# A hard-max attention kernel: load times, step spacing and gather allowance

## The chip, the cores and the metric

The kernel runs on one core of one Trainium2 chip. The metric is the device time of one execution in microseconds (us). A profiled execution comes with a trace; its span, from the first to the last instruction, is a little shorter than the time of the execution.

## The reference

```python
def reference(q, k, v):          # q, k, v: (4, 4096, 128) float32
    logits = np.matmul(q, k.transpose(0, 2, 1))
    best = np.argmax(logits, axis=-1)
    b_idx = np.arange(q.shape[0])[:, None]
    return v[b_idx, best, :].astype(np.float32)
```

For each of 4 × 4096 queries the kernel finds the key with the largest dot product and returns that key's row of v. There is no softmax: the result is a gather.

## The kernel before, in words

The keys of a batch are taken in groups of four rows. From each group the kernel builds sums and differences on TensorE (`trn_half` for the first batch, `unit_k` for the others, L195), so that the largest dot product of a group of four comes out of absolute values and maxima. The queries are cut into 128 tiles of 128 rows (T = 128), 32 to a batch. The work on one tile goes through these stages, spread over several turns of the loop `for it in range(T)` (L792):

- **Screen** (`screen`, `dpart`, `spart`, L228 to L256). TensorE forms 128 × 1024 scores of differences (pd), ScalarE (ACT) takes their absolute value (A, L234, two a tile), TensorE adds A to the scores of sums (psn), ACT writes one half out as 16-bit integers (E, L247). The PSUM pool has four buffers.
- **Fold and top** (`fold` L258, `top` L263). VectorE (DVE) takes the maximum of psn and E into W, whose other half-words hold group numbers, and then the eight largest of 1024 (TOP). Fold of tile it−1 and top of tile it−2 are in turn it.
- **Gather** (`gather`, L271). For four tiles together (two from tile 108 on), DVE computes the indices of the best groups (cand); for each tile one indirect DMA issued by GpSimd (POOL) fetches the three key differences of the best group (kg, L282) from a DRAM copy k16.
- **Dots** (`dots`, L290). DVE multiplies kg by the query (prod, in pieces of two tiles), folds the products twice (p1, p2) and reduces them to D. After each instruction the generator yields. `("dve",)` lets it go on at the next call of `step`; `("wait", 1)` only in the next turn of the loop. `step(it)` (L712) is called twice a turn, once before and once after `top`, and advances one dots generator (two if two are ready) and each pick by an instruction; from TAIL (turn 74) on, picks by two.
- **Pick** (`pick`, L313). For a chunk of eight tiles (four from tile 96 on) five small DVE instructions (mx, near, sel, CNT, win) choose the row within the group; `put_values` then queues one indirect DMA a tile, the value gather (vr, L342), in `late_q`, and a store of the rows by the SP queue.
- **Flags.** Queries whose leading candidates are too close are listed and computed again exactly: `flag_segment` for the first 64 tiles, in the loop from turn 75 on; `flags_last` (L466) for the last 64, after the loop. The latter ends with gathers FK, FQ, FV and a scatter into the output (L541). `late(LATE)` issues that many queued value gathers before FK, `late(1 << 20)` the rest after it.

The order of instructions on every engine is the order of this Python code; nothing reorders it later. POOL issues all gathers and the loads of keys and queries one after the other. How many value gathers go into a turn is decided by `issue(it)` (L743): kg gathers first, one a turn (two when many are queued); then `room` grows by `rate` less `busy` and shrinks by what was issued, capped at 3, and up to two value gathers go out while it is at least 1.

The keys and queries in natural order lie in natk and natq (two buffers each, b % 2). Batch 1's keys are loaded in turns 0 to 7; after that batch b+1's queries are loaded in turns 10 to 16 of a batch, batch b+2's keys in turns 18 to 24. `put_first` (DVE makes kd, SP stores it three times) and `add_rest` (POOL, an accumulating DMA) make k16 for the next batch, in turns 9, 13 and 13, 17 of a batch. `turn_q` transposes queries by SP; `unit_k` runs in the first part of the batch before.

Of the kernel before, what the change touches and what calls it, by code (L numbers as in the profile page):

```python
# [8 lines left out]
FP16 = mybir.dt.float16  # L9
# [12 lines left out]
TAU = 8.0  # L22
NEAR = 0.5
SLOTS = 6
LATE = 4
NKG = 6


# [1 line left out]
def kernel(ctx, tc, q, k, v, out):  # L30
    nc = tc.nc
    B, Sq, D = q.shape
    Sk = k.shape[1]
    P = 128
    NQT = Sq // P
    T = B * NQT
# [9 lines left out]
    bp = ctx.enter_context(tc.tile_pool(name="kq", bufs=1))  # L46
# [10 lines left out]
    k16 = [dr.tile([Sk, 96], FP16, name=f"k16_{b}") for b in range(B)]  # L57
    kT = [bp.tile([P, Sk], FP16, name=f"kT{i}", tag=f"kT{i}") for i in range(2)]
    qT = [bp.tile([P, Sq], FP16, name=f"qT{i}", tag=f"qT{i}") for i in range(2)]
    natk = [bp.tile([P, 2, 16, P], FP16, name=f"natk{i}", tag=f"natk{i}") for i in range(2)]  # L60
    kd = bp.tile([P, 2, 4, 3, P], FP16, name="kd", tag="kd")
    natq = [bp.tile([P, NQT, P], FP16, name=f"natq{i}", tag=f"natq{i}") for i in range(2)]

    def load_k(b, h, x, y):
        kb = k[b].rearrange("(h p n) d -> p h n d", p=P, n=16)
        nc.gpsimd.dma_start(out=natk[b % 2][:, h, x:y], in_=kb[:, h, x:y])  # L66

    def load_q(b, x, y):
        nc.gpsimd.dma_start(out=natq[b % 2][:, x:y], in_=q[b].rearrange("(p t) d -> p t d", p=P)[:, x:y])  # L69

    def put_k(b, h):
        if b >= B:
            return
        src = natk[b % 2][:, h].rearrange("p (g f) d -> p g f d", f=4)
        nc.vector.tensor_tensor(out=kd[:, h], in0=src[:, :, 1:4, :], in1=src[:, :, 0:1, :].to_broadcast([P, 4, 3, P]),
                                op=OP.subtract)
        kb16 = k16[b].rearrange("(h p n) d -> p h (n d)", p=P, n=16)
        nc.sync.dma_start(out=kb16[:, h], in_=kd[:, h].rearrange("p g f d -> p (g f d)"))

    def put_first(b, h):  # L80
        if b >= B:
            return
        src = natk[b % 2][:, h].rearrange("p (g f) d -> p g f d", f=4)
        nc.vector.tensor_scalar(out=kd[:, h, :, 0, :], in0=src[:, :, 0, :], scalar1=-1.0, scalar2=None, op0=OP.mult)
        kb16 = k16[b].rearrange("(r x) d -> r (x d)", x=4).rearrange("(h p g) (f d) -> p h g f d", h=2, p=P, f=3)
        for f in range(3):
            nc.sync.dma_start(out=kb16[:, h, :, f, :], in_=kd[:, h, :, 0, :])

    def add_rest(b, h):
        if b >= B:  # L90
            return
        src = natk[b % 2][:, h].rearrange("p (g f) d -> p g f d", f=4)
        kb16 = k16[b].rearrange("(r x) d -> r (x d)", x=4).rearrange("(h p g) (f d) -> p h g f d", h=2, p=P, f=3)
        nc.gpsimd.dma_start(out=kb16[:, h].rearrange("p g f d -> p g (f d)"), in_=src[:, :, 1:4, :].rearrange("p g f d -> p g (f d)"),
                            accum_op=OP.add)

    def load_part(b, i, n=8):
        if b >= B:
            return
        if i < 8:  # L100
            load_k(b, i // 4, i % 4 * 4, i % 4 * 4 + n)
        else:
            load_q(b, (i - 8) * NQT // 8, (i - 8 + n // 4) * NQT // 8)

    load_k(0, 0, 0, 16)
    load_q(0, 0, 4)
# [14 lines left out]
    identh = cp.tile([P, P], FP16, tag="identh")  # L121
# [73 lines left out]
    def unit_k(b, i):  # L195
        h, u, y = i // 8, i // 2 % 4, i % 2
        x = 2 * (u // 2)
        ps = pp.tile([P, 256], FP32, tag="u", name=f"uk_{b}_{i}")
        for m in (2 * y, 2 * y + 1):
            o = ps[:, (m - 2 * y) * P:(m - 2 * y + 1) * P]  # L200
            nc.tensor.matmul(out=o, lhsT=natk[b % 2][:, h, 4 * m + x, :], rhs=identh, start=True, stop=False)  # L201
            nc.tensor.matmul(out=o, lhsT=natk[b % 2][:, h, 4 * m + x + 1, :],  # L202
                             rhs=identn if u % 2 else identh, start=False, stop=True)
        c = u * 1024 + h * 512 + y * 256
        nc.scalar.activation(out=kT[b % 2][:, c:c + 256], in_=ps, func=AF.Copy)  # L205

    def turn_q(b, x, y):
        nc.sync.dma_start_transpose(out=qT[b % 2][:, x * P:y * P].rearrange("p (t r) -> p t r", r=P),
                                    in_=natq[b % 2][:, x:y, :].rearrange("p t d -> p (t d)"))

    def trn_q(x, y, put):
        ps = pp.tile([P, 512], FP32, tag="u", name=f"tq_{x}")
# [77 lines left out]
    def dots(c, x, m):  # L290
        c0 = chunks[c][0]
        d = D_t[c % 4]
        b = x // NQT
        gap = ("wait", 1) if m == 4 and x < 200 else ("dve",)
        yield "until", lambda: ("kg", x) in done, 2 if m < 4 and x < TAIL else 1
        kg = kg_t.pop(x)
        prod = rp.tile([P, 4, 3, P], FP16, tag="prod", name=f"prod_{x}")[:, 0:m]
        h = min(m, 2)
        for i in range(0, m, h):
            nc.vector.tensor_tensor(out=prod[:, i:i + h], in0=kg[:, i:i + h],  # L300
                                    in1=natq[b % 2][:, x + i - b * NQT:x + i + h - b * NQT, :].unsqueeze(2).to_broadcast([P, h, 3, P]),
                                    op=OP.mult)
            yield gap
        p1 = rp.tile([P, 4, 3, 64], FP16, tag="p1", name=f"p1_{x}")[:, 0:m]
        nc.vector.tensor_tensor(out=p1, in0=prod[:, :, :, 0:64], in1=prod[:, :, :, 64:128], op=OP.add)  # L305
        yield gap
        p2 = rp.tile([P, 4, 3, 32], FP16, tag="p2", name=f"p2_{x}")[:, 0:m]
        nc.vector.tensor_tensor(out=p2, in0=p1[:, :, :, 0:32], in1=p1[:, :, :, 32:64], op=OP.add)  # L308
        yield "dve",
        nc.vector.tensor_reduce(out=d[:, x - c0:x - c0 + m, 1:4], in_=p2, axis=AX_X, op=OP.add)  # L310
        done.update(("dot", i) for i in range(x, x + m))
# [154 lines left out]
    def flags_last(t0, t1, ready, fill, late):  # L466
# [47 lines left out]

        late(LATE)
        get(FK[:, 0, :], k_flat, gb[:, 0:1], B * Sk)
# [226 lines left out]
    def issue(it):  # L743
        n = 0
        clock[0] = it
        put_out(it)
        behind = len([g for g in near_q if g not in marks]) > (2 if it >= TAIL else 4)
        while near_q and (n < 1 + behind or near_q[0] in marks or it >= T - 1):
            g = near_q.pop(0)
            n += g not in marks  # L750
            g()
        if fast and it >= rest[0]:
            fast.pop(0)()
            rest[0] = it + 2
            n += 1
        if it < 16:
            take_late(2 if n == 0 and len(late_q) > 4 else 1)
            return
        b, qt = it // NQT, it % NQT
        busy = 0.7 if qt % 2 == 0 and (10 <= qt < 18 and b + 1 < B or 18 <= qt < 26 and b + 2 < B) else 0.0  # L760
        if qt in (13, 17) and b + 1 < B:
            busy += 1.0
        rate = 2.42 if it < 72 else 2.5 if it < 100 else 2.42
        room[0] = min(room[0] + rate - busy, 3.0) - n
        for i in range(2):
            if room[0] >= 1 and late_q and it < T - 1:
                take_late(1)
                room[0] -= 1
# [16 lines left out]
            start(flag_segment(0, t + 1, lambda: ("cnt", last) in done, lambda: ("out", last) in done), "flags")  # L785

    TAIL = T - 54
    units = []
    for b in range(1, B):
        x = b * NQT  # L790
        units += [(x - 1, x - NQT + (6 + 3 * i // 2 if b == 1 else 1 + 2 * i), unit_k, b, i) for i in range(16)]
    for it in range(T):  # L792
        b, qt = it // NQT, it % NQT
        if it < 8:
            load_part(1, it, 4)
        elif 10 <= qt < 18 and qt % 2 == 0:
            load_part(b + 1, qt - 2)
        elif 18 <= qt < 26 and qt % 2 == 0:
            load_part(b + 2, qt - 18)
        open_units = [u for u in units if u[1] <= it]  # L800
        if open_units:
            u = min(open_units)
            units.remove(u)
            assert it <= u[0]
            u[2](*u[3:])
        if it == 1:
            turn_q(0, 4, 8)
        if it == 40:
            nc.sync.dma_start(out=q32, in_=q[B - 1].rearrange("(p t) d -> p t d", p=P)[:, NQT - 2:NQT])
        if it in (1, 2, 3):  # L810
            turn_q(0, it * 8, it * 8 + 8)
        elif qt >= 16 and qt % 2 == 0 and b + 1 < B:
            turn_q(b + 1, (qt - 16) * 2, (qt - 14) * 2)
        if it > 0:
            screen(it)
        if it >= 1:
            fold(it - 1)
        if it == 1:
            put_k(0, 1)
        if it % NQT in (9, 13):  # L820
            put_first(it // NQT + 1, it % NQT // 13)
        if it % NQT in (13, 17):
            add_rest(it // NQT + 1, it % NQT // 17)
        step(it)
        if it >= 2:
            top(it - 2)
        step(it)
        if it >= 2:
            gathers(it - 2)
        issue(it)  # L830

    def flush():
# [73 lines left out]
```

## Time and profile before

| | before |
|---|---|
| time, median of 3 executions | 443.18 us (442.71 to 443.21) |
| span of the profiled execution | 441.9 us |
| PE busy | 378.9 us |
| DVE busy | 405.9 us |
| ACT busy | 375.6 us |
| POOL busy | 306.2 us |
| kg gathers (L282) | 126, mean 1003 ns |
| value gathers (L342) | 126 and two for the last two tiles, mean 999 ns |
| fold (L260) / top (L264) on DVE | 1306 / 1227 ns mean |
| A (L234) / E (L247) on ACT | 1046 / 1036 ns mean |
| first and last fold start | 16.8 and 404.2 us |

Busy time is the sum of an engine's instructions; two neighbours on DVE or ACT can overlap by about 0.1 us, so a stage is better read from start to start. POOL's time between two gathers is not counted as busy. The page also cuts the span into 40 slices of 11 us, each digit the busy tenths of an engine.

### The profile page before, as it was taken

The page shows a single profiled execution, that of the slowest core. Times are in us where ns is not written, and L with a number is a line of the kernel's source. Part 1 is how long each engine was busy: PE and PEld are TensorE (multiplying, and loading weights), DVE is VectorE, ACT ScalarE, POOL GpSimd, SP SyncE. Part 2 cuts the span into 40 slices and gives each one's busy share as a digit, 9 for nine tenths or more (in the row PEclk, how much of TensorE's full clock was granted, in tenths as well). Part 3 has the DMA queues.
Part 4 walks back from the last instruction along what each step waited for, and adds up shares of the span by engine and source line. Part 5 has one row for each costly group of instructions (what it writes and reads, how often), then busy time and mean ns, then how long its engine had stood idle before and what let it go on. Part 6 is the DMA issues. An engine that isn't in the chain of part 4 may idle for free.

```text
span 441.9 us, 6163 instructions
## 1 busy us (share of the span) xinstructions
PE 378.9 (86%) x1830; PEld 168.0 (38%) x1830; DVE 405.9 (92%) x734; ACT 375.6 (85%) x437; POOL 306.2 (69%) x335
## 2 busy tenths in 40 slices
PE   7999999999999999999998889999889997892100
PEld 4444444444444444444443334443333333330100
DVE  2688999999999999999999999999999999999840
ACT  2899999999999999999998889999989998892000
POOL 8413456677768786777777776777777777777673
PEclk9999999999999999999999999999999999998555
DMA  7933999463326999743336993453322332323432
GB/s 123 202 101 65 157 148 139 106 130 80 108 58 134 180 163 170 147 114 91 84 94 142 173 162 100 96 132 107 85 82 84 90 89 80 88 80 102 122 113 53
DMA packets 52868, 50.54 MB, mean 114 GB/s; under 512 B 34136, under 2 KB 40890, under 8 KB 52832
## 3 DMA queue, kind: packets, MB, share of 16 engines
q0 software_dynamic: 19072, 33.87, 39.2%
q1 hardware_dynamic: 33760, 16.26, 14.5%
q8 instruction: 14, 0.23, 0.2%
q14 instruction: 22, 0.18, 0.2%
HBM read 40.05 MB, written 14.55 MB: 124 GB/s over the span
## 4 chain that ended last, share of the span: by engine, by line
ACT 37%; issue 20%; DVE 13%; PE 12%; POOL 8%; DMA 8%; POOLq 0%; ACTq 0%; DVEq 0%; SPq 0%
ACT A L234 31%; ACT E L247 6%; DVE TOP L264 4%; PE psn L225 4%; POOL vr L342 4%; PE pd L225 4%; POOL kg L282 4%; DVE W L260 4%; PE psn L244 3%; DMA vr<-in_v_dram,win 3%; DMA natk<-in_k_dram 2%; DMA out_dram<-vr 1%; DMA kg<-k,cand 1%; DVE prod L300 1%; DMA vr<-in_v_dram,win_w 1%
## 5 line engine op out<-in xcount | busy, mean ns | idle before, releaser
L234 ACT ACTIVATE A<-pd 128x1024 f16<-128x1024 f32 x256 | 260.8, 1046 | 12.5 <-PE pd L225 12.0
L282 POOL DMA_INDIRECT kg<-k,cand x126 | 126.4, 1003 | 80.0 <-DVE cand L276 48.7
L260 DVE SCALAR_TENSOR_TENSOR W<-psn,E 128x1024 int16<-128x1024 f32 x128 | 167.1, 1306 | 7.4 <-ACT E L247 5.3
L225 PE MATMUL psn<-kT,qT 128*128 128x512 f16 x512 | 151.9, 378 | 11.4 <-ACT A L234 4.0
L225 PE MATMUL pd<-kT,qT 128*128 128x512 f16 x512 | 151.9, 379 | 8.7 <-ACT A L234 8.2
L264 DVE MAX8 TOP<-W 128x8 f32<-128x1024 f32 x128 | 157.0, 1227 | 0.0
L225 PEld LDWEIGHTS <-qT 128*128 128x128 f16 x1024 | 97.9, 97 | 151.8 <-issue 62.0
L342 POOL DMA_INDIRECT vr<-in_v_dram,win x126 | 125.9, 999 | 40.0 <-issue 36.1
L244 PE MATMUL psn<-A,identh 128*128 128x512 f16 x512 | 152.1, 378 | 0.0
L247 ACT ACTIVATE E<-psn 128x1024 int16<-128x1024 f32 x128 | 132.6, 1036 | 2.3 <-PE psn L244 1.5
L244 PEld LDWEIGHTS <-identh 128*128 128x128 f16 x512 | 49.6, 97 | 60.7
L300 DVE TENSOR_TENSOR prod<-kg,natq 128x768 f16<-128x768 f16 x63 | 34.8, 554 | 0.4 <-DMA kg<-k,cand 0.4
L205 ACT ACTIVATE kT<-uk 128x256 f16<-128x256 f32 x48 | 20.6, 429 | 1.5 <-PE uk L202 1.5
L305 DVE TENSOR_TENSOR p<-prod 128x768 f16<-128x768 f16 (+1 forms) x36 | 18.1, 502 | 0.1
L310 DVE TENSOR_REDUCE D<-p 128x12 f32<-128x384 f16 (+1 forms) x36 | 17.7, 492 | 0.1
L201 PE MATMUL uk<-identh,natk 128*128 128x128 f16 x96 | 15.8, 218 | 0.0
L484 PE MATMUL fp_e<-n_e,tri 128*128 128x1 f32 x2 | 0.6, 364 | 13.5 <-DVE n_e L482 13.5
L202 PEld LDWEIGHTS <-natk 128*128 128x128 f16 x96 | 9.3, 97 | 7.2 <-issue 5.1
L308 DVE TENSOR_TENSOR p<-p 128x384 f16<-128x384 f16 (+1 forms) x36 | 11.9, 330 | 0.1
L66 POOL DMA_DIRECT2D natk<-in_k_dram x19 | 11.3, 599 | 0.8 <-POOLq L890 0.8
L201 PEld LDWEIGHTS <-natk 128*128 128x128 f16 x96 | 9.3, 98 | 5.6
L69 POOL DMA_DIRECT2D natq<-in_q_dram x15 | 9.2, 614 | 0.0
(152 smaller groups left out, 140.1 us busy)
## 6 DMA issues: line engine op xcount, KB each, us to landing
out_dram<-vr SPq DMA_DIRECT2D x31, 256.0 KB, 2.1
natq<-in_q_dram POOLq DMA_DIRECT2D x12, 256.0 KB, 5.3
natk<-in_k_dram POOLq DMA_DIRECT2D x10, 256.0 KB, 4.5
k<-kd SPq DMA_DIRECT2D x18, 128.0 KB, 3.7
k<-natk POOLq DMA_DIRECT2D x6, 384.0 KB, 6.4
kg<-k,cand POOLq DMA_INDIRECT x126, 3.0
vr<-in_v_dram,win POOLq DMA_INDIRECT x126, 2.7
natk<-in_k_dram POOLq DMA_DIRECT2D x8, 128.0 KB, 5.7
```

Of the source, the lines that this page charges most:

```text
L201: nc.tensor.matmul(out=o, lhsT=natk[b % 2][:, h, 4 * m + x, :], rhs=identh, start=True, stop=False)
L205: nc.scalar.activation(out=kT[b % 2][:, c:c + 256], in_=ps, func=AF.Copy)
L225: nc.tensor.matmul(out=ps[:, n * 512:(n + 1) * 512], lhsT=qT[b % 2][:, qt * P:(qt + 1) * P], rhs=kT[b % 2][:, u * 1024 + n * 512:u * 1024 ...
L234: nc.scalar.activation(out=A, in_=ps, func=AF.Abs)
L244: nc.tensor.matmul(out=ps[:, n * 512:(n + 1) * 512], lhsT=identh, rhs=A[:, n * 512:(n + 1) * 512], start=False, stop=True)
L247: nc.scalar.activation(out=E, in_=ps, func=AF.Relu, scale=QSCALE)
L260: nc.vector.scalar_tensor_tensor(out=W_t[t % NW].bitcast(I16)[:, 1::2], in0=ps, scalar=QSCALE, in1=E, op0=OP.mult, op1=OP.max)
L264: nc.vector.max(out=TOP[:, t, :], in_=W_t[t % NW].bitcast(FP32))
L282: near_q.append(lambda j=j: nc.gpsimd.indirect_dma_start(out=kg[:, j].rearrange("p f d -> p (f d)"), out_offset=None, in_=k16[t0 // NQT], ...
L300: nc.vector.tensor_tensor(out=prod[:, i:i + h], in0=kg[:, i:i + h], in1=natq[b % 2][:, x + i - b * NQT:x + i + h - b * NQT, :].unsqueeze(2 ...
L305: nc.vector.tensor_tensor(out=p1, in0=prod[:, :, :, 0:64], in1=prod[:, :, :, 64:128], op=OP.add)
L342: late_q.append(lambda j=j: nc.gpsimd.indirect_dma_start(out=vr[:, j, :], out_offset=None, in_=v_flat, in_offset=IOA(ap=win[:, i + j:i + j ...
```

## The change

The buffers natk and natq get a third copy (b % 3). The loads of batches 1 to 3 follow a table, `load_plan(batch, first turn, gap, pieces, what)`; `put_first` and `add_rest` get turns of their own by batch. In the old code batch 3's keys were loaded in turns 50 to 56 and its queries in 74 to 80, its `put_first` in 73 and 77, `add_rest` in 77 and 81. `dots` waits a turn between instructions only for x < 80, and in the last 20 turns `step` is called a third time. The allowance has other rates. LATE goes from 4 to 5.

```diff
-LATE = 4
+LATE = 5
...
-    natk = [... for i in range(2)]
+    natk = [... for i in range(3)]
...
-    natq = [... for i in range(2)]
+    natq = [... for i in range(3)]
...
-        gap = ("wait", 1) if m == 4 and x < 200 else ("dve",)
+        gap = ("wait", 1) if m == 4 and x < 80 else ("dve",)
...
-        busy = 0.7 if qt % 2 == 0 and (10 <= qt < 18 and b + 1 < B or 18 <= qt < 26 and b + 2 < B) else 0.0
-        if qt in (13, 17) and b + 1 < B:
+        busy = 0.5 if plan.get(it) else 0.0
+        if it in (46, 50, 66, 70):
             busy += 1.0
-        rate = 2.42 if it < 72 else 2.5 if it < 100 else 2.42
+        rate = 2.45 if it < 72 else 2.65 if it < 80 else 2.45 if it < 96 else 2.6 if it < 104 else 2.45 if it < 112 else 2.6
...
+    load_plan(1, 0, 1, 4, "k")
+    load_plan(1, 8, 2, 8, "q")
+    load_plan(2, 18, 2, 8, "k")
+    load_plan(2, 30, 3, 8, "q")
+    load_plan(3, 42, 3, 8, "k")
+    load_plan(3, 54, 3, 8, "q")
...
-        if it < 8:
-            load_part(1, it, 4)
-        elif 10 <= qt < 18 and qt % 2 == 0:
-            load_part(b + 1, qt - 2)
-        elif 18 <= qt < 26 and qt % 2 == 0:
-            load_part(b + 2, qt - 18)
+        for piece in plan.get(it, []):
+            piece()
...
-        if it % NQT in (9, 13):
-            put_first(it // NQT + 1, it % NQT // 13)
-        if it % NQT in (13, 17):
-            add_rest(it // NQT + 1, it % NQT // 17)
+        for b1, x, y in ((1, 9, 13), (2, 41, 46), (3, 56, 66)):
+            for h in range(2):
+                if it == x + 4 * h:
+                    put_first(b1, h)
+                if it == y + 4 * h:
+                    add_rest(b1, h)
         step(it)
         if it >= 2:
             top(it - 2)
         step(it)
+        for _ in range(1 if it >= T - 20 else 0):
+            step(it)
```

More of the change, by code (lines that the diff above doesn't have):

```diff
@@ L59 @@
     qT = [bp.tile([P, Sq], FP16, name=f"qT{i}", tag=f"qT{i}") for i in range(2)]
-    natk = [bp.tile([P, 2, 16, P], FP16, name=f"natk{i}", tag=f"natk{i}") for i in range(2)]
+    natk = [bp.tile([P, 2, 16, P], FP16, name=f"natk{i}", tag=f"natk{i}") for i in range(3)]
     kd = bp.tile([P, 2, 4, 3, P], FP16, name="kd", tag="kd")
-    natq = [bp.tile([P, NQT, P], FP16, name=f"natq{i}", tag=f"natq{i}") for i in range(2)]
+    natq = [bp.tile([P, NQT, P], FP16, name=f"natq{i}", tag=f"natq{i}") for i in range(3)]
     def load_k(b, h, x, y):
         kb = k[b].rearrange("(h p n) d -> p h n d", p=P, n=16)
-        nc.gpsimd.dma_start(out=natk[b % 2][:, h, x:y], in_=kb[:, h, x:y])
+        nc.gpsimd.dma_start(out=natk[b % 3][:, h, x:y], in_=kb[:, h, x:y])
     def load_q(b, x, y):
-        nc.gpsimd.dma_start(out=natq[b % 2][:, x:y], in_=q[b].rearrange("(p t) d -> p t d", p=P)[:, x:y])
+        nc.gpsimd.dma_start(out=natq[b % 3][:, x:y], in_=q[b].rearrange("(p t) d -> p t d", p=P)[:, x:y])
     def put_k(b, h):
@@ L73, in put_k @@
             return
-        src = natk[b % 2][:, h].rearrange("p (g f) d -> p g f d", f=4)
+        src = natk[b % 3][:, h].rearrange("p (g f) d -> p g f d", f=4)
         nc.vector.tensor_tensor(out=kd[:, h], in0=src[:, :, 1:4, :], in1=src[:, :, 0:1, :].to_broadcast([P, 4, 3, P]),
@@ L82, in put_first @@
             return
-        src = natk[b % 2][:, h].rearrange("p (g f) d -> p g f d", f=4)
+        src = natk[b % 3][:, h].rearrange("p (g f) d -> p g f d", f=4)
         nc.vector.tensor_scalar(out=kd[:, h, :, 0, :], in0=src[:, :, 0, :], scalar1=-1.0, scalar2=None, op0=OP.mult)
@@ L91, in add_rest @@
             return
-        src = natk[b % 2][:, h].rearrange("p (g f) d -> p g f d", f=4)
+        src = natk[b % 3][:, h].rearrange("p (g f) d -> p g f d", f=4)
         kb16 = k16[b].rearrange("(r x) d -> r (x d)", x=4).rearrange("(h p g) (f d) -> p h g f d", h=2, p=P, f=3)
@@ L95, in add_rest, with load_plan @@
                             accum_op=OP.add)
[L97 to L103, printed above, removed]
+    plan = {}
+    def load_plan(b, first, gap, n, what):
+        for i in range(32 // n):
+            x, y = i * n, i * n + n
+            plan.setdefault(first + i * gap, []).append(
+                lambda b=b, x=x, y=y: load_k(b, x // 16, x % 16, x % 16 + n) if what == "k" else load_q(b, x, y))
     load_k(0, 0, 0, 16)
@@ L200, in unit_k @@
             o = ps[:, (m - 2 * y) * P:(m - 2 * y + 1) * P]
-            nc.tensor.matmul(out=o, lhsT=natk[b % 2][:, h, 4 * m + x, :], rhs=identh, start=True, stop=False)
-            nc.tensor.matmul(out=o, lhsT=natk[b % 2][:, h, 4 * m + x + 1, :],
+            nc.tensor.matmul(out=o, lhsT=natk[b % 3][:, h, 4 * m + x, :], rhs=identh, start=True, stop=False)
+            nc.tensor.matmul(out=o, lhsT=natk[b % 3][:, h, 4 * m + x + 1, :],
                              rhs=identn if u % 2 else identh, start=False, stop=True)
@@ L208, in turn_q @@
         nc.sync.dma_start_transpose(out=qT[b % 2][:, x * P:y * P].rearrange("p (t r) -> p t r", r=P),
-                                    in_=natq[b % 2][:, x:y, :].rearrange("p t d -> p (t d)"))
+                                    in_=natq[b % 3][:, x:y, :].rearrange("p t d -> p (t d)"))
     def trn_q(x, y, put):
@@ L300, in dots @@
             nc.vector.tensor_tensor(out=prod[:, i:i + h], in0=kg[:, i:i + h],
-                                    in1=natq[b % 2][:, x + i - b * NQT:x + i + h - b * NQT, :].unsqueeze(2).to_broadcast([P, h, 3, P]),
+                                    in1=natq[b % 3][:, x + i - b * NQT:x + i + h - b * NQT, :].unsqueeze(2).to_broadcast([P, h, 3, P]),
                                     op=OP.mult)
```

## The prediction

> **What bounds the kernel now.** I read the page's 40 slices first, then the busy time of each stretch of 40 us, then the single instructions of DVE and POOL in order of time. The slices:
>
> ```profile
> DVE  2688999999999999999999999999999999999840
> ACT  2899999999999999999998889999989998892000
> POOL 8413456677768786777777776777777777777673
> ```
>
> DVE stays at nine tenths to the end of the tile loop; ACT drops below it from slice 22 on. The stretches (us, then busy us of PE, PEld, DVE, ACT, POOL, the clock, DMA):
>
> ```profile
> 160.00:200.00 40.00, 39.29 (x192) 17.55 (x191) 40.00 (x59) 40.00 (x50) 29.94 (x32) 1.00 0.75 144
> 320.00:360.00 40.00, 36.21 (x151) 14.61 (x151) 39.83 (x68) 36.64 (x39) 29.78 (x30) 1.00 0.29 83
> 400.00:442.00 42.00, 2.47 (x12) 1.63 (x10) 23.08 (x114) 0.48 (x1) 25.64 (x26) 0.56 0.33 94
> ```
>
> At 160:200 DVE and ACT are both full: eight tiles take 23.4 us, 2.92 each. From tile 72 (228 us) the flag segment and, from 96, smaller picks load DVE alone: eight tiles then take 27.3, 24.6, 23.9, 26.6, 24.2, 26.5 and 23.1 us, and when I add the start-to-start times of DVE's own instructions per block they leave less than 0.9 us unexplained in each. So **DVE's list of work sets the loop, from 40 to 404 us**. POOL shows 30 of 40 busy, but each gather is followed by 0.30 us called "issue", so a gather costs 1.25 us (1.30 near the end): 30 × 1.3 is 39, nearly full too. After 404 us only POOL is long:
>
> ```profile
> 413.88 1.00 POOL L342 DMA_INDIRECT vr<-in_v_dram,win  x1 [0.30 <-issue]
> 417.17 1.05 POOL L512 DMA_INDIRECT FK<-in_k_dram,gb_e  x1 [2.29 <-DVE row_e L509]
> ...
> 422.43 1.00 POOL L342 DMA_INDIRECT vr<-in_v_dram,win  x1 [0.30 <-issue]
> ...
> 431.62 1.00 POOL L342 DMA_INDIRECT vr<-in_v_dram,win_w  x1 [0.30 <-issue]
> 432.92 0.99 POOL L512 DMA_INDIRECT FV<-in_v_dram,xw_fe  x1 [0.30 <-issue]
> 437.69 1.02 POOL L541 DMA_INDIRECT out_dram<-FV,rowk_e  x1 [3.77 <-DMA out_dram<-vr]
> ```
>
> POOL stands still 2.29 us before the first FK gather, then runs four FK/FQ and eight leftover value gathers (422.43 to 431.62, 1.30 apart) before FV, although DVE had FV's index at 426.74. The last scatter follows the last value gather by 6.07 us. **The tail ends as late as the value gathers left over.**
>
> **What the Trainium skill says.** "VectorE: DVE Perf Modes", section "The DRAIN you can't avoid": the next instruction waits until the pipe is empty, but one that is not held starts earlier, and a semaphore costs nothing extra. The trace agrees with the early start and not with the free semaphore:
>
> ```profile
> 372.94 0.16 DVE L320 TENSOR_REDUCE mx<-D 128x4 f32<-128x16 f32 x1
> 373.02 0.55 DVE L300 TENSOR_TENSOR prod<-kg,natq 128x768 f16<-128x768 f16 x1
> ...
> 410.56 0.16 DVE L320 TENSOR_REDUCE mx<-D 128x4 f32<-128x16 f32 x1
> 410.75 0.18 DVE L323 SCALAR_TENSOR_TENSOR near<-D,mx 128x16 f32<-128x16 f32 x1
> ```
>
> An mx followed by its reader costs 0.19 us to the next start, followed by a stranger 0.08. Likewise p1 to p2 0.39 against 0.26, prod to p1 0.58 against 0.46, sel to CNT 0.20 against 0.09. "DMA: Bandwidth & Descriptors", section "SWDGE vs HWDGE vs iDMA", has one queue for software-made DMAs; the trace shows POOL's loads and gathers strictly in turn. The same page's section "Anatomy of one DMA — SWDGE (gpsimd) path" puts the fixed cost near 2 us; here a kg gather takes a median 3.0 us to land (2.6 to 7.4), which I use.
>
> **The change, part by part.**
>
> 1. *Third buffers.* POOL's waits name no reader of natk or natq, so they remove no wait: 0.
>
> 2. *Loads and accumulations moved.* The same 28 loads of batches 1 to 3 and six accumulations stay. A q load holds POOL 0.9 us (234.30 to the next start at 235.21), an accumulation 1.65 (1.35 plus 0.30). Batch 3's four q loads and two accumulations, 4 × 0.9 + 2 × 1.65 = 6.9 us, leave tiles 74 to 81 for 54 to 70. There DVE sets the pace and its products do not wait for POOL (all prod waits sum to 0.4 us in the run), so leaving brings 0. Arriving: tiles 42 to 71 then ask POOL for 60 × 1.25 + 8 × 0.9 + 4 × 1.65 = 88.8 us in 30 × 2.92 = 87.7. A lag of about 1 us is hidden: there the product starts 4.7 to 10.6 us after its last kg gather, which lands in about 3. DVE's two kd instructions (0.19 each) move from a DVE-bound stretch to another: 0. The six SP stores of put_first are passed by transposes with slack of several tiles: 0.
>
> 3. *Allowance.* Followed tile by tile through `issue`, the old rule leaves five value gathers when the loop ends and 5 + 8 around FK, exactly the trace. The new rates leave two. Value gathers issued by the end of tile 95: 86 before, 85 after; in tiles 96 to 127: 29 and 33. With LATE one higher, six instead of five lie before FK and **four instead of eight after it: 4 × 1.30 = 5.2 us less** between FK and the end. FV would start at 427.7, still after its index (426.74); the last scatter, 6.07 us behind the last value gather, moves the same 5.2.
>    POOL must place five more gathers between tile 96 and FK: 6.5 us. Its idle there is 3.2 us (waits for cand, beyond 0.30 each, between 304 and 404) plus 2.0 before FK, so 1.3 us is short, unless DVE is later anyway.
>
> 4. *Two steps a tile (x from 80) and a third step (last 20 tiles).* DVE's list is the same; only its order changes. Written out from the code, 20 more pairs stand directly one behind the other with the second reading the first: 12 within picks (0.11 each), 2 prod-p1 (0.12), 6 p1-p2 (0.13): **1.3 + 0.24 + 0.78 = 2.3 us**, nearly all in tiles 104 to 127, where DVE is the bound: on the path. Second, the work becomes lumpy: nine of the tiles 80 to 127 have less than 2.75 us for DVE (two of them only fold and top, 2.33), where before had none; 2.75 is the shortest regular fold-to-fold time seen. The trace shows no lighter tile. Bounds: 0 (ACT, 2.72 a tile there, has got ahead in the heavy tile in front) to the sum of what is missing to 2.75, 1.7 us. I take 0.4, since the heavy neighbours give ACT its lead. No gain is possible here, since no DVE idle is there to be removed. "Picks later" I find in no edit: the cuts and the group sizes are unchanged.
>
> 5. *What waits more.* With 2.7 us more on DVE the POOL shortfall of 1.3 is covered, so kg gathers are not later against their products (slack in this stretch 3.7 to 4.7 us against some 3 to 4 of landing). I take 0; upper bound 1.3.
>
> Sum against the profiled span: 441.9 − 5.2 + 2.3 + 0.4 = 439.4. The other runs' median is 443.18 us, 1.3 above that span; minus 2.5 gives **440.7 us**.
>
> **The rivals.**
>
> *The packing is free* (the pairs hide in DVE's waits for ACT or PE): only the tail gain and POOL's shortfall of 0 to 1.3 remain, −5.2 to −3.9: 438.0 to 439.3. Against it: from tile 72 on DVE waits for hardly anything.
>
> *POOL's lag eats it*: at rates of 2.6 two tiles ask for five gathers, 6.5 us, where the last block's tiles take 2 × 2.9; if kg gathers fall behind their 3.7 us of slack, products wait, and everything behind them on DVE (top, then fold, so PSUM and TensorE). With the upper ends, 2.3 + 1.7 + 1.3 − 5.2 = +0.1: 443.3. For it: one product already waited 0.4 us at 385 us.
>
> *Slower: light tiles starve DVE.* If after a heavy tile ACT and PE have no lead, because a fold holds the PSUM buffer that the next scores need, each of the nine light tiles is as long as an average tile of 112 to 119, 3.31 us, instead of their 23.0 us in sum: + 6.8. Then −5.2 + 2.3 + 6.8 = +3.9: 447.1. It decides from 0.42 us of idle per light tile on (9 × 0.42 + 2.3 − 5.2 = +0.9). Against it: ACT needs only 2.72.
>
> **How the numbers follow.** Free packing 0.22, the forecast (439.3 to 442.3) 0.57, lag 0.12 (within 442.3 to 444.1), starving 0.09. About 0.2% (0.9 us) is what a measurement can tell from no change. Faster 0.22 + 0.57 = 0.79, same 0.12, slower 0.09. The range leaves out starving, the upper part of the lag case and the lowest end: 437.9 to 442.9.
>
> **What would show it.** Right: four value gathers between the last FK and FV, POOL's 2.29 us before FK gone, FV about 10.5 us after FK instead of 15.75; the last fold 2 to 3 us later than 404.2, with mx-near starts 0.19 apart in tiles 117 to 126. Wrong: the last fold no later (free), DVE idle before folds in tiles 92, 96, 104, 108, 111, 112 (starving), or before products after 350 us (lag); more than four value gathers behind FK would break step 3.

## The result, and the profile after

| | before | after |
|---|---|---|
| time, median | 443.1 us (442.71 to 443.21) | 444.75 us (444.24 to 445.6, four runs) |
| ratio, with 95% interval | | 1.0041 (1.0022 to 1.006) |
| span of the profiled execution | 441.9 us | 442.4 us |

The change makes the kernel slower by 0.4%; I had predicted 440.7 us. The slices and the stretches of the page after, in the columns of the prediction:

```profile
DVE  2688999999999999999999999999999999999950
ACT  2899999999999999999998889999989997883000
POOL 8424456777777677787777757777767777777770
```

```profile
160.00:200.00 40.00, 39.30 (x192) 17.48 (x190) 40.00 (x61) 39.93 (x49) 31.64 (x33) 1.00 0.85 163
320.00:360.00 40.00, 35.71 (x151) 14.49 (x150) 39.69 (x68) 35.71 (x38) 29.81 (x30) 1.00 0.31 89
400.00:442.00 42.00, 4.45 (x22) 2.44 (x19) 25.12 (x117) 2.02 (x3) 23.37 (x24) 0.59 0.31 91
```

In the loop DVE is full in the same stretches; what there is to find lies at the end. The last POOL slice is 0, where it was 3: POOL's last instruction now comes earlier in a span that ends later. POOL's instructions at the end (start, duration, operation, idle before and its releaser):

```profile
419.40 1.06 POOL L512 DMA_INDIRECT FK<-in_k_dram,gb_e  x1 [0.42 <-DVE row_e L509]
...
424.66 0.99 POOL L342 DMA_INDIRECT vr<-in_v_dram,win  x1 [0.30 <-DMA FQ<-in_q_dram,row_e]
425.96 0.99 POOL L342 DMA_INDIRECT vr<-in_v_dram,win  x1 [0.30 <-issue]
427.26 1.07 POOL L342 DMA_INDIRECT vr<-in_v_dram,win_w  x1 [0.31 <-issue]
428.64 0.99 POOL L342 DMA_INDIRECT vr<-in_v_dram,win_w  x1 [0.30 <-issue]
429.94 1.00 POOL L512 DMA_INDIRECT FV<-in_v_dram,xw_fe  x1 [0.30 <-issue]
434.51 1.02 POOL L541 DMA_INDIRECT out_dram<-FV,rowk_e  x1 [3.58 <-DMA out_dram<-vr]
```

Four value gathers stand between the last FK and FV instead of eight, FV follows FK by 10.54 us, and the scatter starts 3.2 us earlier than before (437.69). This is what was predicted, or a little better (10.5 us, and 2.5 us earlier). But the span ends 7.87 us after the scatter starts; before it was 4.19. Start to start:

| stretch | before | after | difference |
|---|---|---|---|
| start to last fold (L260) | 404.18 | 406.47 | +2.29 |
| last fold to first FK | 12.99 | 12.93 | −0.06 |
| first FK to FV | 15.75 | 10.54 | −5.21 |
| FV to scatter | 4.77 | 4.57 | −0.20 |
| scatter to end of span | 4.19 | 7.87 | +3.68 |
| sum | 441.88 | 442.38 | +0.50 |

The execution that was traced before took 443.8 us, 0.7 more than the median, so the first line of the table, +2.29, is too small by 0.6 us; the experiments below show it.

No busy instruction lies behind the scatter, so the page's groups show nothing there. One has to ask for the instructions of the program's last line, queue instructions among them. Columns: smallest, median and largest duration in ns, first and last start in us. Before:

```profile
L901 POOLq DRAIN  x3: 46/109/3253, 437.5 to 441.6; - x3
```

and after:

```profile
L907 POOLq DRAIN  x3: 46/109/7255, 434.3 to 442.1; - x3
```

The first of these is POOL's end-of-program drain, a queue instruction at the last line of the program. The trace shows when it starts and ends, not what it does. It starts with the scatter (0.23 us ahead of its record) and lasts 7.255 us instead of 3.253. What the SP queue waits for at that line (total us, times, longest us), before:

```profile
SPq L901 <- DMA out_dram<-FV,rowk_e: 3.6, 1, 3.6
SPq L901 <- PEq L901: 0.7, 2, 0.5
```

and after:

```profile
SPq L907 <- PEq L907: 4.3, 2, 3.8
SPq L907 <- DMA out_dram<-FV,rowk_e: 3.6, 1, 3.6
```

The landing of the scatter takes SP 3.6 us in both. Before, the drain ended at 440.71 us, 1.17 us ahead of the end of the span; SP was through with the landing and its own last queue instructions at 441.04, later than the drain, so the drain was hidden. After, SP is through at 437.96, but POOL drains until 441.54, and SP goes on at 441.71. The long wait of SP is put down to PE; its end, 0.17 us behind POOL's drain, says that it is a wait for POOL. The drain is 4.00 us longer and the end 3.68 us later behind the scatter, so about 0.3 us of it had been to spare. **The tail that was won is given back as a new wait behind it.**

### The profile page after: what moved, and what is told of

It is laid out like the page before. It is cut to its first block, busy times and chain, and to the rows that moved or that the text cites. A ratio compares the mean times of both kernels' runs of the same rounds, so it can differ in the third digit from the quotient of the medians.

```text
span 442.4 us, 6167 instructions
## 1 busy us (share of the span) xinstructions
PE 378.3 (86%) x1830; PEld 168.0 (38%) x1830; DVE 407.8 (92%) x734; ACT 375.8 (85%) x437; POOL 303.1 (69%) x335
## 4 chain that ended last, share of the span: by engine, by line
ACT 33%; DVE 27%; issue 18%; PE 15%; DMA 4%; POOL 1%; POOLq 0%; ACTq 0%; DVEq 0%; SPq 0%
ACT A L234 27%; DVE TOP L264 12%; DVE W L260 8%; ACT E L247 6%; PE psn L225 6%; PE psn L244 4%; PE pd L225 4%; DVE prod L300 2%; DMA natk<-in_k_dram 2%; DMA FK<-in_k_dram,gb_e 1%; DVE p L305 1%; DVE p L308 1%; DVE D L310 1%; DMA vr<-in_v_dram,win_w 1%; DMA out_dram<-vr 0%
## 5 line engine op out<-in xcount | busy, mean ns | idle before, releaser
L260 DVE SCALAR_TENSOR_TENSOR W<-psn,E 128x1024 int16<-128x1024 f32 x128 | 166.6, 1302 | 7.4 <-ACT E L247 5.3
L342 POOL DMA_INDIRECT vr<-in_v_dram,win x126 | 123.3, 979 | 40.1 <-issue 35.4
```

The lines of the kernel that those rows point to most:

```text
L260: nc.vector.scalar_tensor_tensor(out=W_t[t % NW].bitcast(I16)[:, 1::2], in0=ps, scalar=QSCALE, in1=E, op0=OP.mult, op1=OP.max)
L342: late_q.append(lambda j=j: nc.gpsimd.indirect_dma_start(out=vr[:, j, :], out_offset=None, in_=v_flat, in_offset=IOA(ap=win[:, i + j:i + j ...
```

## The experiments

The question was what makes the drain long. *Theory A*: POOL's software-made DMAs leave work that is done at a fixed time, about 441.5 us, so that an earlier scatter meets a longer drain and no shortening of the tail can help. *The rivals*: it comes with the moved loads and accumulations, or with the packing of the dots.

### LATE 5 alone (x1)

```diff
-LATE = 4
+LATE = 5
```

> The kernel before with LATE 5 alone: the last fold stays at 404.2 us, seven value gathers follow the last FK instead of eight, so FV comes at 431.6 and the last scatter at about 436.4 us, 1.3 earlier. Theory A (POOL has work behind its records that is worked off at its own pace, so its final drain ends at a nearly fixed time, 440.7 to 441.5 us, whatever the scatter does): span 441.9, time 443.1, no gain; the final drain is 4.5 us long instead of 3.25. Theory B (the final drain's extra length belongs to the changed kernel's own tail or main loop): the drain stays near 3.25 us, span 440.6, time 441.8.

Measured: 441.94 us (441.47 to 442.71) against 443.31 of before, ratio 0.9971 (0.9963 to 0.9979). Seven value gathers lie behind FK, and FV follows FK by 14.49 us instead of 15.75. The scatter starts at 435.59, 2.1 us earlier than before, 0.7 of it because the last fold does (403.47). That 0.7 is no work of LATE, which acts after the loop. The trace of before starts its first fold 0.3 us later than x1's (16.77 against 16.48), and it holds the one wait of DVE for a gather:

```profile
DVE prod L300 <- DMA kg<-k,cand: 0.4, 1, 0.4
```

Neither x1, x2 nor v2 (below), which keep the old steps as well, has this wait, and their last folds start at 403.47, 403.55 and 403.48. So 403.5, not 404.2, is what the old steps usually give.

```profile
L901 POOLq DRAIN  x3: 46/109/3252, 435.4 to 439.5; - x3
```

The drain moves with the scatter and keeps its 3.25 us. Theory A, of a fixed time, falls, and one gather taken from behind FK is worth its 1.3 us (1.26 from FK to FV, 1.4 in the time).

### The change without its packing (x2), the packing alone (x3)

```diff
-        gap = ("wait", 1) if m == 4 and x < 80 else ("dve",)
+        gap = ("wait", 1) if m == 4 and x < 200 else ("dve",)
...
-        for _ in range(1 if it >= T - 20 else 0):
-            step(it)
```

> The changed kernel with the step spacing of before (one instruction a turn for groups of four, no third step): the last fold falls back from 406.5 to 404.2 us; six value gathers follow the last FK, FV at 430.3, last scatter at about 435.1 us. Theory A: the final drain still ends at 440.7 to 441.5, time 443 to 444. Theory B with the packing as the cause: drain ends 2 us after the scatter, span 439.3, time 440.5.

x3 is the kernel before with the opposite edit.

> The kernel before with the closer steps alone: 2.3 us more on DVE, last fold at 406.5 us; seven value gathers after the last FK, FV at 433.9, last scatter at 438.7 us. Both theories: end set by the scatter's landing or by the drain, span 442.9 to 443.5, time 444.1 to 444.7; if the 2.3 us of the packing were no loss on the whole, time 443.1.

x2: 444.29 us (443.56 to 445.75), ratio 1.0026 (1.0017 to 1.0035). Last fold 403.55, scatter 434.42, and the drain is long:

```profile
L905 POOLq DRAIN  x3: 46/109/7253, 434.2 to 442.0; - x3
```

x3: 444.85 us (444.1 to 445.24), ratio 1.0034 (1.0021 to 1.0047). Last fold 406.39, seven value gathers behind FK, scatter 438.69, and the drain is short:

```profile
L903 POOLq DRAIN  x3: 46/109/3253, 438.5 to 442.6; - x3
```

So the packing has no part in the drain. What it costs is read from traces that, up to the last fold, differ in it alone. The last folds of x1 and of x3,

```profile
403.47 1.29 DVE L260 SCALAR_TENSOR_TENSOR W<-psn,E 128x1024 int16<-128x1024 f32 x1
```

```profile
406.39 1.30 DVE L260 SCALAR_TENSOR_TENSOR W<-psn,E 128x1024 int16<-128x1024 f32 x1
```

are 2.9 us apart, and so are those of x2 (403.55) and of the change (406.47). The packing costs 2.9 us of DVE, not 2.3. x3's time says the same: it is 1.5 us above before, although one gather less behind FK saves 1.4 (14.36 us from FK to FV instead of 15.75), and it lies above the range that was expected.

x2 shows one thing more: without the packing six gathers stay behind FK, not four (13.06 us from FK to FV instead of 10.54). The later DVE of the full change pays for two gathers, 2.5 us for 2.9; the times, 444.75 and 444.29, lie within the spread of their runs.

### Fewer value gathers (x4)

The value gathers of tiles 32 to 63, 32 of them, are left out; plain reads by SP of other rows take their place, so the output of these tiles is not the reference's.

```diff
-        for j in range(m):
+        if chunks[c][0] in (32, 40, 48, 56):
+            b, qt = chunks[c][0] // NQT, chunks[c][0] % NQT
+            nc.sync.dma_start(out=vr[:, 0:m], in_=v[b].rearrange("(p t) d -> p t d", p=P)[:, qt + i:qt + i + m])
+        for j in range(0 if chunks[c][0] in (32, 40, 48, 56) else m):
             late_q.append(...)
```

> The changed kernel, with the value rows of tiles 32 to 63 not gathered but read in order by SP's queue, so that 32 of POOL's gathers are left out in the middle of the run (the output of these tiles is then not the reference's). Scatter at 434.5 us as in the changed kernel. Theory A: POOL's hidden backlog is smaller by 32 gathers, the final drain shrinks from 7.25 us to about 3.25, span 438.7, time 440.7. Theory B: drain stays at 7 us, time 444.7.

Measured: 445.14 us (444.91 to 445.33), ratio 1.0044 (1.0027 to 1.0061); scatter at 434.00.

```profile
L910 POOLq DRAIN  x3: 46/109/8968, 433.8 to 443.3; - x3
```

Neither expectation holds: with 32 gathers fewer the drain is longer, 8.97 us. That it clears a backlog that grows with the number of POOL's DMAs falls too.

### Part by part, by the drain's duration

The next kernels ran on chips on which the kernel before itself took 524 to 535 us in the median; DVE's folds waited 38.6 us for psn there (y3), against 1.6 before. Why is open. Their times are too spread to be used: w0 came to 1.0009 of before (0.9913 to 1.0106), w2 to 1.0088 (0.9985 to 1.0191), w3 to 1.0149 (1.0025 to 1.0273). What is used is the duration of the drain, which did not change with the chip: the kernel with the loads back gave 3.222, 3.226 and 3.222 us there and 3.211 where the kernel before took 443 us.

*Loads and accumulations back in before's turns, the rest of the change kept* (y3, z0, w0, v0). The table `plan` stays for the allowance; the loads follow a second one, `turns`. Only 16 of the 28 loads differ in their turn: the queries of batches 1 to 3 and the keys of batch 3.

```diff
...
+    load_plan(1, 0, 1, 4, "k", turns)
+    load_plan(1, 10, 2, 8, "q", turns)
+    load_plan(2, 18, 2, 8, "k", turns)
+    load_plan(2, 42, 2, 8, "q", turns)
+    load_plan(3, 50, 2, 8, "k", turns)
+    load_plan(3, 74, 2, 8, "q", turns)
...
-        for piece in plan.get(it, []):
+        for piece in turns.get(it, []):
...
-        for b1, x, y in ((1, 9, 13), (2, 41, 46), (3, 56, 66)):
+        for b1, x, y in ((1, 9, 13), (2, 41, 45), (3, 73, 77)):
```

> The changed kernel with the loads, put_first and add_rest of all batches back in the turns of before; third buffers, allowance, steps and LATE as changed, so every gather stands where it stands in the changed kernel. Theory L (the order of the loads among POOL's DMAs sets the length of POOL's final drain): drain 3.25 us instead of 7.25, last scatter at 434.5, span 438.4, time 440.4 to 440.8. Theory G (the order of the gathers, or the third buffers, sets it): drain 7.25 us, time 444.7.

> The kernel of y3_loads_back once more: the changed kernel with the loads, put_first and add_rest back in the turns of before. Theory L: POOL's final drain 3.2 us, last fold 406.5, last scatter 434.5, span 438.4, time 440.4 to 440.8 (about 4 us under the changed kernel's 444.75). Theory G, left with no support by y3's drain of 3.22 us: 444.7.

The drain of y3:

```profile
L915 POOLq DRAIN  x3: 46/109/3222, 520.2 to 524.3; - x3
```

*Moved loads and third buffers alone* (z3, w3): before's allowance, steps and LATE 4, with the loads, `put_first` and `add_rest` of the change.

> The kernel before with the third buffers and the moved loads, put_first and add_rest alone; allowance, steps and LATE of before. Theory L: last fold 404.2, eight value gathers after the last FK, scatter 437.7 as before, but a final drain of 7.25 us instead of 3.25: span 445.6, time 446.9 (3.6 us slower than before). If the drain needs more than the order of the loads: 443.3.

> The kernel before with the third buffers and the moved loads, put_first and add_rest alone. Theory L: last scatter at 437.7 as before, drain 7.25 us, time 446.9 us, ratio 1.008. If the loop gains from the moved loads: the last fold before 403.5 and a time of 446 or less.

The drain of w3 (z3: 7.253):

```profile
L905 POOLq DRAIN  x3: 46/109/7257, 515.8 to 523.6; - x3
```

With the loads back the drain is 3.2 us; with the moved loads and third buffers alone it is 7.25. The third buffers are in y3 too. **The moved loads and accumulations make the drain long, and no other part of the change does.** (This part alone was not timed on a chip where the kernel before takes 443 us.)

*Loads moved, accumulations and `put_first` back* (r1): only the last line of the diff above.

> The changed kernel with put_first and add_rest alone back in the turns of before; the loads stay where the change puts them. If the place of the accumulating transfers sets the drain: 3.2 us. If the place of the loads does: 7.25 us. Any third value says that both count.

```profile
L907 POOLq DRAIN  x3: 46/109/7469, 523.4 to 531.5; - x3
```

The loads in their new turns are enough for the long drain. By its own expectation the third value, 7.47 us, says that the accumulations count as well: putting them back adds 0.2 us. The loads back with the accumulations moved, or a part of the 16 loads, was not tried.

*More or fewer instructions on POOL, on top of the change*: eight more gathers ahead of the loop (y1, with one iota for their index), eight more memsets (y2), 64 value gathers left out and read by SP (y5; the output of tiles 32 to 95 is not the reference's).

```diff
+    row0 = cp.tile([P, 1], U32, tag="row0")
...
+    for i in range(8):
+        xtra = cp.tile([P, P], FP32, name=f"xtra{i}", tag=f"xtra{i % 2}")
+        nc.gpsimd.indirect_dma_start(out=xtra, out_offset=None, in_=v_flat, in_offset=IOA(ap=row0, axis=0))
```

```diff
+    row0 = cp.tile([P, 8], FP32, tag="row0")
+    for i in range(8):
+        nc.gpsimd.memset(row0[:, i:i + 1], 0.0)
```

> The changed kernel with eight more gathers of 128 rows, into tiles that nobody reads, on POOL before the tile loop. Theory R (the final drain depends on [...]the number and sizes of all DMAs before it): the drain changes; taking 32 gathers away gave +1.715 us, so linearly about -0.43, 6.8 us, and by another amount if it wraps. Theory P (only the tail's own DMAs or the place of POOL's instructions in memory count): 7.25 us, or any other value that eight non-DMA instructions give too.

> The changed kernel with eight small memsets on POOL before the tile loop, no DMA more. Theory R: drain stays at 7.25 us. Theory P (place of the instructions in memory): the drain changes by about as much as with eight gathers.

> The changed kernel with the value rows of tiles 32 to 95 read in order by SP, so that 64 of POOL's gathers are left out (the output of these tiles is not the reference's). Theory R, linear: drain 7.25 + 2 x 1.715 = 10.7 us, unless it wraps, which would show as a drop by a fixed amount. Theory A, still: the drain shrinks. If the length only knows two or three values without relation to the count: neither.

The drains of y1, y2 and y5, one fence each:

```profile
L912 POOLq DRAIN  x3: 46/109/3508, 543.1 to 547.3; - x3
```

```profile
L910 POOLq DRAIN  x3: 46/109/7265, 533.5 to 541.6; - x3
```

```profile
L910 POOLq DRAIN  x3: 46/109/6367, 470.5 to 477.4; - x3
```

Eight gathers at 13 to 28 us, over 500 us ahead of the end, bring the drain from 7.25 to 3.51 us; eight memsets leave it (7.265). 32 gathers fewer gave 8.97, 64 fewer 6.37; these two kernels also add reads by SP, y1 adds none. So the drain depends on the DMAs that POOL has issued in the whole run, on their number and on the turns of the loads, and not on how many lie shortly before it: with the loads in either place it stays within 0.05 us over the different allowances, steps and LATE. The rule behind it is not found. The linear form of theory R fails (6.8 and 10.7 us were expected of y1 and y5), theory P falls with the memsets, and whether anything wraps was not tested.

### The allowance alone, with LATE 5 (z1) and 6 (z2, w2)

The loads are back and the packing is undone, so that DVE's order is before's and POOL's allowance is the new one.

> The kernel before with the new allowance and LATE 5, loads and steps as before (third buffers stay): last fold 404.0, six value gathers after the last FK, FV at 429.8, last scatter 434.6, drain 3.2 us: span 438.5, time 440.6. If the step packing paid for itself, it would be slower than z0_loads_back_again; by its 2.3 us on DVE less two gathers of 1.3 us they should lie within 0.5 us of each other.

> As z1_allowance_alone with LATE 6: five value gathers after the last FK, 1.3 us less there, but seven before it fill POOL's wait for FK's index and put FK off by 0.5 to 0.7 us: span 437.8, time 439.9. If FK is put off by the whole 1.3 us: 440.6.

On the chips above, LATE 5 leaves six value gathers behind FK, LATE 6 five; both drains are 3.212 us. That led to the last two kernels.

### Two kernels that take the drain away (v0, v2)

v0 is the change with the loads back (the diff above). v2 is the kernel before with the new allowance and LATE 6; loads and steps stay before's, and the third buffers and the table `plan`, which the allowance reads, are those of the change:

```diff
-LATE = 4
+LATE = 6
...
-        busy = 0.7 if qt % 2 == 0 and (10 <= qt < 18 and b + 1 < B or 18 <= qt < 26 and b + 2 < B) else 0.0
+        busy = 0.5 if plan.get(it) else 0.0
-        if qt in (13, 17) and b + 1 < B:
+        if it in (46, 50, 66, 70):
...
-        rate = 2.42 if it < 72 else 2.5 if it < 100 else 2.42
+        rate = 2.45 if it < 72 else 2.65 if it < 80 else 2.45 if it < 96 else 2.6 if it < 104 else 2.45 if it < 112 else 2.6
```

> The kernel of w0_loads_back once more, for its time on a chip where the kernel before takes 443 us. Theory L: drain 3.2 us, last fold 406.5, last scatter 434.5, span 438.4, time 440.4 to 440.8 us, ratio 0.994. If the moved loads were worth something in the loop: above 441.5.

> The kernel before with the new allowance and LATE 6 (third buffers stay, loads and steps as before), for its time on a chip where the kernel before takes 443 us: last fold 404, five value gathers after the last FK, drain 3.2 us; span 437.8, time 439.9 us, ratio 0.9925. If the seventh gather before FK puts FK off by its whole 1.3 us: 440.6 us.

v0: 441.01 us (439.88 to 441.85) against 442.98, ratio 0.9956 (0.994 to 0.9972), 3.7 us under the change; its drain is 3.211 us, and the span ends 4.19 us after the scatter starts. v2: **439.5 us (439.29 to 439.76) against 443.13, ratio 0.9917 (0.9903 to 0.993)**, better than both kernels. POOL at the end of v2:

```profile
416.71 1.08 POOL L513 DMA_INDIRECT FK<-in_k_dram,gb_e  x1 [0.31 <-DVE XD L570]
...
428.62 1.00 POOL L513 DMA_INDIRECT FV<-in_v_dram,xw_fe  x1 [0.30 <-issue]
433.21 1.02 POOL L542 DMA_INDIRECT out_dram<-FV,rowk_e  x1 [3.59 <-DMA out_dram<-vr]
```

```profile
SPq L913 <- DMA out_dram<-FV,rowk_e: 3.6, 1, 3.6
SPq L913 <- PEq L913: 0.7, 2, 0.5
```

SP's two waits are those of the kernel before again. In the stretches of the table, against before: last fold −0.7 (403.5), fold to FK +0.2, FK to FV −3.84 (11.91), FV to scatter −0.18, scatter to end 0 (4.19); together −4.5, to a span of 437.4. The 0.7 belongs to the traced execution of before (see x1); without it −3.8 is left, and the difference of the times is 3.6. POOL's wait ahead of FK is gone (0.31 us left), and the two gathers more that go there put FK off by 0.2 us.

## Why the prediction was wrong

- **Third buffers, 0.** No run speaks against it, and none tests them alone.
- **Loads and accumulations moved, 0: this step failed.** I followed the loads through what stands around them in the loop (POOL's pace, DVE's products, SP's stores), and there they cost nothing: the fold of tile 72 starts at 228.3 us instead of 228.0, and the last fold at 406.47 against 406.36 in v0. Their price, 3.7 us, falls at the very end, in POOL's drain, which they lengthen from 3.25 to 7.25 us. The drain stood in the trace of before, with about 0.3 us to spare against the landing of the scatter; I had not looked at the queue instructions of the last line. Why the turns of the loads set the length of the drain stays open.
- **Allowance, 5.2 us less.** Right in the middle, wrong at its end. Four gathers fewer, 5.21 us from FK to FV, 10.54 instead of my 10.5, and the scatter earlier by all that the sum gave. "Moves the same 5.2" took it for granted that the end follows the scatter at 4.2 us. It does so in x1, x3, v0 and v2, and not where the loads are moved. Beside that, the counts by stage were off by eight (78 and 77 by the end of tile 95, then 37 and 41); the difference of four, which the step used, is right. The 1.3 us that POOL would be short without a later DVE were 2.5 (x2: two gathers more behind FK).
- **Two steps a tile and a third step, 2.3 + 0.4.** The sum, 2.7, is near the 2.9 us that x1 and x3, or x2 and the change, show; the parts are not. The 0.4 for light tiles is 0: from 256 us to the last fold, in x1, x3 and the change, the trace shows no wait of DVE at all. The pairs cost more than 2.3. From the fold of tile 80 to the last one x3 is 2.8 us longer than x1. Of this about 2.5 us lie in 22 more pairs whose second instruction reads the first: the 20 that I had listed, and one top before its cand and one D before its mx, which I had not. The rest is spread thinly. That the two errors nearly cancel is luck. The pairs of a pick in the change follow each other by 0.18 to 0.21 us:

```profile
385.31 0.15 DVE L320 TENSOR_REDUCE mx<-D 128x4 f32<-128x16 f32 x1
385.49 0.18 DVE L323 SCALAR_TENSOR_TENSOR near<-D,mx 128x16 f32<-128x16 f32 x1
385.70 0.17 DVE L327 TENSOR_TENSOR sel<-near,iota 128x16 f32<-128x16 f32 x1
385.91 0.17 DVE L329 TENSOR_REDUCE CNT<-sel 128x4 f32<-128x16 f32 x1
```

  Such pairs show what a reader costs over a stranger, about 0.1 us. They do not separate the semaphore from the wait for the result, so "not with the free semaphore" said more than these lines show.
- **What waits more, 0.** Right: no product waits for its kg gather. The one wait of 0.4 us in the trace of before is missing in x1, x2 and v2 as well, so the change did not remove it, and it was no sign for the lag. That the 6.5 us of gathers need DVE's lateness is shown by x2 and z1: without it six gathers, not four, stay behind FK.
- **The rivals.** Free packing falls with x3. POOL's lag would show as products waiting, and they don't. Starving light tiles would show before folds, and DVE waits for nothing there. (The last of the block times in the prediction, 23.1 us, covers seven tiles, not eight; nothing rests on it.) The change is slower through a fourth mechanism, which I had not on the list: I had not asked what else ends at the end.

With the loads back the rest of the forecast nearly holds: v0 takes 441.01 us where 440.7 was predicted, 2.0 us under before where I had 2.5. The error that decides is one term, 0 in place of 3.7 us.

## What to carry to other kernels

When a tail is shortened, list everything that runs beside its last piece, queue instructions and end-of-program drains included, with the time that each has to spare: here the spare was about 0.3 us, and the page's busy times did not show it. A step that costs nothing where it stands can still lengthen something hundreds of us later, so after moving DMAs compare the end of the trace, not only their neighbourhood. Take a small difference from traces that differ in one edit alone: one traced execution can be 0.7 us off, as before's was. And try the parts one by one: the allowance with LATE 6 gains 3.6 us, the whole change without the long drain 2.0.

## What the runs showed of the hardware

- POOL's drain at the end of a program took 3.2 to 9.0 us in these kernels, for one order of POOL's DMAs the same to within 0.015 us on different chips (3.211 to 3.226 with the loads back, 7.255 and 7.265 in the change and y2, 7.253 and 7.257 in z3 and w3). Eight gathers issued over 500 us earlier changed it by 3.7 us. It showed little or nothing at the end up to 3.5 us (scatter to end 4.19 us at 3.25, 4.29 at 3.51); SP waits 3.6 us for the landing of the last scatter meanwhile. At 6.37 the end came 2.8 us later (6.96).
- An instruction on DVE that reads the result of the one just before it started about 0.1 us later than a stranger did (mx before near 0.19, before another 0.07); 22 more such pairs came to about 2.5 us of the loop.
